# A transformer trunk on one NeuronCore: the last 256 output channels with tokens stationary, and two gate tiles ahead of the second branch

## The chip, the cores and the metric

The kernel runs on one core of a Trainium2 chip. A core has a matrix engine (TensorE, here PE), a vector engine (VectorE, DVE), an engine for functions of one operand (ScalarE, ACT), a general engine (GpSimd, POOL) and a queue engine (SyncE, SP). They share the on-chip memory SBUF; PE writes into the banks of PSUM, which DVE and ACT read. DMA engines move data between DRAM and SBUF; a transfer is issued from the queue of SP, ACT or POOL. The metric is the device time of one execution in microseconds, as the median of several.

## The reference

One layer for 256 tokens of 2048 channels in fp32. A token mixer of three branches comes first, then a gated MLP, then a last RMS norm:

```
h = rms_norm(x, mix_norm)
(u_a, q_b, f_b, i_b, og_b, cx_c, v_c, o_c, ig_c, fg_c, gates) = split(h @ w_in)
y_a = s5_mixer(u_a, ...)                    # state space model, 512 channels
y_b = hgrn2_mixer(q_b, f_b, i_b, og_b, ...) # gated recurrence, 6 heads of 128
y_c = mlstm_mixer(cx_c, v_c, o_c, ...)      # matrix memory, 4 heads of 192
merged = sigmoid(g_a) * (y_a @ w_a) + sigmoid(g_b) * (y_b @ w_b) + sigmoid(g_c) * (y_c @ w_c)
x = x + merged @ w_out
up = causal_dwconv(rms_norm(x, ffn_norm) @ w_up, 3 taps)   # 2 x 5632 channels
x = x + (silu(up[:5632]) * up[5632:]) @ w_down
return rms_norm(x, final_norm)              # x * rsqrt(mean(x*x) + 1e-6) * final_norm
```

## The kernel before

Everything is kept with channels on the 128 partitions and the 256 tokens along the free axis; a channel tile is 128 channels by 256 tokens, and x has 16 of them. Products are made in three parts for precision: each fp32 operand is split into a high and a low part (type fp32r), and high x high, high x low and low x high are summed in a bank. Weights are split on the chip: a job loads up to 2048 columns of a weight matrix into a buffer `raw` (three of them, issued on SP), and each sub-job of up to 1024 columns has its high part `wh` written by ACT (line 117) and its low part `wl` by DVE (line 128), three buffers each. PE multiplies at line 148.

There are two ways round. In `form_a` (line 334) the weights are stationary and the tokens move; the wide form sends both parts of the moving operand past the high weights in one 512-wide product and adds one 256-wide product for the low weights. In `form_b` (line 383) 128 tokens are stationary and the weights move, and the result has tokens on the partitions.

The order of the instructions is written by the program itself: a list of jobs in the order of the calls at the end of `hybrid_trunk` (lines 1535 to 1563), worked through by `run_jobs` (line 271) with the splits two sub-jobs and the loads two jobs ahead. Between pieces of a job a function `pump` (line 223) advances generators, which are the smaller work (norms, recurrences, heads) cut into steps. A clock model `ck` with costs per instruction decides how far they go; it sets the order only. Each engine then works through its own queue in order and waits on semaphores.

In the middle, the names are these. `project_tail` makes the last two token projections (og and o). Behind them come the products of the second branch with its weights `w_bb`: six jobs of two output tiles, each tile one sub-job of 768 columns with 18 products. A gate tile (`gate_tile`, line 1237) is a wide product over 16 channel tiles whose result, times the row factor `R1`, goes through a sigmoid and is kept in a page until the branch is merged; branch b keeps its gates on the pages 8 and 9, and so does branch c after it. Meanwhile the mLSTM generator turns the input and forget gates `gif` into the tile `rows` (Abs, Exp, Ln on ACT, with function tables to load between them), and the four heads follow.

At the end, `w_down_tiles` makes the 16 channel tiles of the down projection, 44 contraction tiles each, tiles 0 to 14 in the wide form and tile 15 with three 256-wide products per contraction tile. Each is added to x; its squares are summed into `ACC` on POOL, and x is multiplied by `final_norm`, all beside the next tile's products. After tile 15, `row_stats` sums the squares over partitions with a product with ones, makes 1/sqrt with Ln, Exp and one Newton step over 256 columns, and `finish` multiplies all 16 tiles by the result in six pieces (three tiles of the last one on POOL) and stores them from the queues of SP and ACT.

## Time and profile before

| | us |
|---|---|
| median of three runs | 1558.77 (1557.72 to 1559.37) |
| the profiled execution | 1557.51 |
| its span in the trace | 1555.7 |
| PE busy in the span | 1533.6 (99%) |
| DVE, ACT, POOL busy | 1085.2, 879.3, 93.0 |

The span runs from the first to the last thing that the trace has; the time of the execution is a little longer. An engine's busy time is that of its instructions, and for a matmul it is a modelled one: a product 256 wide has a record of some 0.28 us, while the next one starts about 0.12 us after it, so start times tell more than lengths. A chain of waits is followed back from the last instruction to whatever released each step. An instruction that waits is listed with the engine and instruction that ended its wait.

### The profile page before, as it was taken

The page shows a single profiled execution, that of the slowest core. Times are in us where ns is not written, and L with a number is a line of the kernel's source. Part 1 is how long each engine was busy: PE and PEld are TensorE (multiplying, and loading weights), DVE is VectorE, ACT ScalarE, POOL GpSimd, SP SyncE. Part 2 cuts the span into 40 slices and gives each one's busy share as a digit, 9 for nine tenths or more (in the row PEclk, how much of TensorE's full clock was granted, in tenths as well). Part 3 has the DMA queues.
Part 4 walks back from the last instruction along what each step waited for, and adds up shares of the span by engine and source line. Part 5 has one row for each costly group of instructions (what it writes and reads, how often), then busy time and mean ns, then how long its engine had stood idle before and what let it go on. Part 6 is the DMA issues. An engine that isn't in the chain of part 4 may idle for free.

```text
span 1555.7 us, 25413 instructions
## 1 busy us (share of the span) xinstructions
PE 1533.6 (99%) x10166; PEld 1398.6 (90%) x10166; DVE 1085.2 (70%) x1668; ACT 879.3 (57%) x1287; POOL 93.0 (6%) x178
## 2 busy tenths in 40 slices
PE   9999999999999999999999999999999999999996
PEld 9999999998899888898888888888888888888886
DVE  7887986778744666686667777777777776545454
ACT  5456666566645477454556555555555555444442
POOL 7400000000000000000110000000000000000010
PEclk9999999999999999999999999999999999999998
DMA  7555454345555524466555555555555555555552
GB/s 306 200 181 168 171 205 163 137 162 179 173 173 193 180 102 173 162 233 217 190 187 184 187 185 187 186 187 190 189 187 190 190 190 183 186 195 180 196 179 99
DMA packets 43014, 285.07 MB, mean 183 GB/s; under 512 B 4944, under 2 KB 5328, under 8 KB 13200
## 3 DMA queue, kind: packets, MB, share of 16 engines
q1 hardware_dynamic: 40464, 274.19, 51.0%
q0 software_dynamic: 1568, 7.28, 1.4%
q10 hardware_dynamic: 864, 2.00, 0.3%
q8 instruction: 79, 1.29, 0.3%
q14 instruction: 39, 0.32, 0.1%
HBM read 281.34 MB, written 2.10 MB: 182 GB/s over the span
## 4 chain that ended last, share of the span: by engine, by line
PE 95%; POOL 2%; DMA 1%; DVE 1%; ACT 1%; issue 1%; DVEq 0%; SPq 0%; ACTq 0%
PE mp L148 90%; PE xp L148 4%; DMA xT<-x 1%; PE xp L157 0%; POOL s_cs L128 0%; ACT wh L117 0%; POOL s5pw L134 0%; DVE wl L128 0%; POOL s_z L128 0%; DVE x L128 0%; POOL s_th L128 0%; POOL s5pw L136 0%; DVEq L1677 0%; POOL xm L134 0%; ACT rows L117 0%
## 5 line engine op out<-in xcount | busy, mean ns | idle before, releaser
L128 DVE TENSOR_TENSOR wl<-raw,wh 128x1024 fp32r<-128x1024 f32 (+2 forms) x534 | 633.8, 1188 | 416.6 <-ACT wh L117 412.6
L117 ACT ACTIVATE wh<-raw 128x1024 fp32r<-128x1024 f32 (+2 forms) x534 | 549.9, 1031 | 613.1 <-PE mp L148 498.7
L148 PE MATMUL mp<-HX,wh 128*128 128x512 f32 (+1 forms) x3072 | 871.6, 353 | 3.1 <-DVE merged L128 1.5
L148 PE MATMUL mp<-HX,wl 128*128 128x256 f32 x2496 | 672.7, 280 | 0.0
L148 PEld LDWEIGHTS mp<-HX,wh 128*128 128x128 f32 x3072 | 527.1, 188 | 79.0 <-issue 2.7
L148 PEld LDWEIGHTS mp<-HX,wl 128*128 128x128 f32 x2496 | 465.8, 188 | 10.2
L148 PE MATMUL mp<-g,wh 128*128 128x512 f32 (+1 forms) x748 | 245.2, 380 | 0.0
L148 PE MATMUL mp<-g,wl 128*128 128x256 f32 x704 | 195.0, 281 | 0.0
L148 PEld LDWEIGHTS mp<-g,wh 128*128 128x128 f32 x748 | 136.4, 188 | 27.4
L148 PE MATMUL mp<-wh,HX 128*128 128x256 f32 (+1 forms) x768 | 139.5, 282 | 0.0
L148 PEld LDWEIGHTS mp<-g,wl 128*128 128x128 f32 x704 | 132.3, 188 | 1.3
L148 PEld LDWEIGHTS mp<-wh,HX 128*128 128x128 f32 x768 | 119.4, 189 | 0.2 <-issue 0.2
L148 PE MATMUL mp<-wl,HX 128*128 128x256 f32 (+1 forms) x384 | 108.1, 281 | 0.5 <-DVE wl L128 0.5
L148 PE MATMUL mp<-m,wh 128*128 128x512 f32 x256 | 88.8, 395 | 0.0
L140 DVE SCALAR_TENSOR_TENSOR upc<-up,cols,upc 128x255 f32<-128x255 f32 (+1 forms) x176 | 84.6, 481 | 3.1
L148 PEld LDWEIGHTS mp<-wl,HX 128*128 128x128 f32 x384 | 72.3, 188 | 0.8 <-DVE wl L128 0.7
L148 PE MATMUL mp<-m,wl 128*128 128x256 f32 x256 | 69.2, 280 | 0.0
L117 ACT ACT_TABLE_LOAD x46 | 59.0, 1283 | 0.8
L117 ACT ACTIVATE upc<-up,cols 128x256 f32<-128x256 f32 x88 | 53.0, 602 | 11.1 <-DVE up L128 11.0
L148 PEld LDWEIGHTS mp<-m,wh 128*128 128x128 f32 x256 | 47.1, 188 | 10.0
L148 PEld LDWEIGHTS mp<-m,wl 128*128 128x128 f32 x256 | 48.1, 188 | 1.3
L128 POOL TENSOR_TENSOR ACC<-ACC,sq 128x256 f32<-128x256 f32 x28 | 33.4, 1194 | 261.4 <-ACT sq L117 261.4
(320 smaller groups left out, 1330.6 us busy)
## 6 DMA issues: line engine op xcount, KB each, us to landing
raw<-w_in SPq DMA_DIRECT2D x88, 1024.0 KB, 4.8
raw<-w_up SPq DMA_DIRECT2D x88, 1024.0 KB, 4.9
raw<-w_down SPq DMA_DIRECT2D x32, 1024.0 KB, 5.0
raw<-w_out SPq DMA_DIRECT2D x16, 1024.0 KB, 4.9
raw<-w_down SPq DMA_DIRECT2D x16, 768.0 KB, 4.2
raw<-w_bb SPq DMA_DIRECT2D x8, 768.0 KB, 4.2
raw<-w_bc SPq DMA_DIRECT2D x8, 768.0 KB, 4.3
raw<-w_ba SPq DMA_DIRECT2D x4, 1024.0 KB, 4.9
```

Of the source, the lines that this page charges most:

```text
L117: nc.scalar.activation(out=out, in_=in_, func=func, **kw)
L128: e.tensor_tensor(out=out, in0=in0, in1=in1, op=op)
L140: nc.vector.scalar_tensor_tensor(out=out, in0=in0, scalar=s, in1=in1, op0=op0, op1=op1)
L148: nc.tensor.matmul(out, lhsT, rhs, start=start, stop=stop)
```

## The change

Two parts. First, the last two channel tiles of the down projection (256 channels) are no longer made with weights stationary. `last_tiles` makes them with tokens stationary: for each of two token tiles one bank of 128 tokens by 256 channels, over 44 contraction tiles with three products each. The weights come in eleven sub-jobs of four contraction tiles; a sub-job marked A is multiplied for both token tiles, one marked R for token tile 0 only, and its split weights are kept in `HH` and `HL` until token tile 0 is complete. The residual x of these channels is added by products with the identity matrix. The squares of the first 14 channel tiles are summed over partitions to one column per token tile (`rest_means`), and the squares of the last 256 channels are summed along the row by ACT. So in `tail` the norm of a token tile is a column of 128 numbers. It multiplies the new channels directly, and a product with the identity spreads it over partitions for the 14 old tiles, which are read from SBUF with this factor from a bank. Each token tile has its own stores; tile 0's tail is a generator among the products left for tile 1. The output array has another layout, and `final_norm` of the last channels comes in as rows (`finr`).

Second, two of branch c's gate tiles stand ahead of the second branch's jobs, the other ten where the twelve stood; branch c's first six gates are on page 15 in place of page 8, and the pages are told apart by branch.

```diff
             if part is None or i == part:
                 nc.sync.dma_start(out=job["raw"][:, c0:c0 + n], in_=job["src"][:, c0:c0 + n])
-    def split(job, c0, n):
+    def split(job, c0, n, to=None):
         raw = job["raw"]
-        wh = sb([P, RAW // 2], F32R, "wh", bufs=3)
-        wl = sb([P, RAW // 2], F32R, "wl", bufs=3)
+        wh = to[0] if to else sb([P, RAW // 2], F32R, "wh", bufs=3)
+        wl = to[1] if to else sb([P, RAW // 2], F32R, "wl", bufs=3)
...
@@ -1242,8 +1242,8 @@
                 if key == "a" and m == 4:
                     yield from wait_for("us2")
                 if (m - 4 if key == "a" else m) % 6 == 0:
-                    merged["page", m // 6] = page(at[m // 6], [P, 6, T], name="gates")
-                s = merged["page", 0 if key == "a" else m // 6][:, m % 6, :]
+                    merged["page", key, m // 6] = page(at[m // 6], [P, 6, T], name="gates")
+                s = merged["page", key, 0 if key == "a" else m // 6][:, m % 6, :]
             merged[key, m] = s
             if wide:
                 total(s, ps)
...
@@ -1411,37 +1411,123 @@
         def evac(m):
             def f(ps):
                 x = v["x"][m // 8][:, m % 8, :]
-                if m < KT - 1:
-                    tt(x, x, ps[:, 0], ADD, after=ck.t["pe"] - 2.6)
-                    tt(x, x, ps[:, 1], ADD)
-                else:
-                    tt(x, x, ps, ADD, after=ck.t["pe"])
-                if m < KT - 1:
-                    yield
-                sq = squares(x, m)
-                if m < KT - 1:
-                    yield
-                    act(x, x, AF.Copy, scale=col("fin", m))
-                else:
-                    yield from row_stats([ACC, sq])
+                tt(x, x, ps[:, 0], ADD, after=ck.t["pe"] - 2.6)
+                tt(x, x, ps[:, 1], ADD)
+                yield
+                squares(x, m)
+                yield
+                act(x, x, AF.Copy, scale=col("fin", m))
+                if m == KT - 3:
+                    gens.append(("r1", rest_means(ck.t["pool"])))
             return f
-        for m in range(KT):
-            form_a(a["w_down"][m], g_parts, evac(m), nk=FT, before=table_for_ln if m == 8 else None, flush=m == 0,
-                   wide=m < KT - 1)
+        for m in range(KT - 2):
+            form_a(a["w_down"][m], g_parts, evac(m), nk=FT, before=table_for_ln if m == 8 else None, flush=m == 0, wide=True)
+        last_tiles()
+    end = {}
+    def rest_means(t):
+        yield from until("pe", t)
+        bank = yield from side()
+        for i in range(NT):
+            mm(bank[:, i:i + 1], ACC[:, i * P:(i + 1) * P], ones[:, 0:1], True, True)
+        yield
+        end["rest"] = small([P, NT], "rest")
+        end["rest_at"] = ts(end["rest"], bank[:, :NT], 1.0 / D, MULT, EPS, ADD, after=ck.t["pe"])
+        shut(bank)
+    def last_tiles():
+        kept, order = [], "AAARARARARA"
+        hi, lo = (x.rearrange("p k t -> p (k t)") for x in (HH, HL))
+        def products(i, k, w_h, w_l, first=False, last=False):
+            ps = end[i]
+            g = [x[:, i * P:(i + 1) * P] for x in (g_parts(k)[:, 0], g_parts(k)[:, 1])]
+            mm(ps, g[0], w_h, first, False)
+            if first:
+                for c in range(2):
+                    mm(ps[:, c * P:(c + 1) * P], v["x"][1][:, 6 + c, i * P:(i + 1) * P], ident, False, False)
+            mm(ps, g[0], w_l, False, False)
+            mm(ps, g[1], w_h, False, last)
+        def sub(n):
+            def fn(wh, wl):
+                if n == 0:
+                    for i in range(NT):
+                        end[i] = main_ps()[:, :T]
+                w = [(4 * n + k, wh[:, k * T:(k + 1) * T], wl[:, k * T:(k + 1) * T]) for k in range(4)]
+                ends = n == len(order) - 1
+                for i in range(NT if order[n] == "A" else 1):
+                    if i:
+                        yield
+                    for j, x in enumerate(w):
+                        products(i, *x, first=n == 0 and j == 0, last=i == 0 and ends and j == 3)
+                    if ends and i == 0:
+                        gens.append(("r1", tail(0, ck.t["pe"])))
+                if order[n] == "R":
+                    kept.extend(w)
+                if ends:
+                    for j, x in enumerate(kept):
+                        yield
+                        products(1, *x, last=j == len(kept) - 1)
+                return []
+            return fn
+        def before():
+            ck.table = TABLES[AF.Ln]
+            end["fin"] = page(15, [P, T], name="finr")
+            nc.gpsimd.dma_start(out=end["fin"], in_=a["finr"])
+        at, n = 0, 0
+        while n < len(order):
+            m = min(2, len(order) - n)
+            job = add_job(a["w_dl"][:, at:at + m * 1024], m * 1024, [(1024 * k, 1024, sub(n + k)) for k in range(m)],
+                          before=before if n == 0 else None)
+            job["to"] = {}
+            for k in range(m):
+                if order[n + k] == "R":
+                    c = order[:n + k].count("R") * 1024
+                    job["to"][k] = (hi[:, c:c + 1024], lo[:, c:c + 1024])
+            at, n = at + m * 1024, n + m
+    def tail(i, t):
+        y = sb([P, RAW], F32, "raw", bufs=3, name="y")
+        ps = end[i]
+        sq, acc, w, r = scratch(name="sq"), small([P, 1], f"acc{i}"), small([P, 1], f"lw{i}"), small([P, 1], f"lr{i}")
+        var = small([P, 1], f"lv{i}")
+        t = act(sq, ps, AF.Square, accum_out=acc, after=max(t, end["rest_at"]))
+        tv = ts(var, acc, 1.0 / D, MULT, end["rest"][:, i:i + 1], ADD, after=t)
+        act(w, acc, AF.Ln, scale=1.0 / D, bias=end["rest"][:, i:i + 1])
+        t = act(r, w, AF.Exp, scale=-0.5)
+        stt(w, r, -0.5, r, MULT, MULT, after=max(t, tv))
+        tt(w, w, var, MULT)
+        t = stt(r, w, 1.5, r, ADD, MULT)
+        queues = (nc.sync, nc.scalar)
+        stt(y[:, D - T:D], ps, r[:, 0:1], end["fin"], MULT, MULT)
+        queues[1].dma_start(out=a["out"][i, :, D - T:], in_=y[:, D - T:D])
+        yield from until("pe", t)
+        bank = yield from side()
+        R = bank[:, :P]
+        mm(R, r[:, 0:1].broadcast_to([P, P]), ident, True, True, after=t)
+        t = ck.t["pe"]
+        at = 0
+        for g, n in enumerate((4, 4, 3, 3) if i == 0 else (2, 3, 3, 4, 2)):
+            o = at % 8
+            tt(y[:, at * P:(at + n) * P].rearrange("p (m t) -> p m t", t=P),
+               v["x"][at // 8][:, o:o + n, i * P:(i + 1) * P], bc(R.unsqueeze(1), [P, n, P]), MULT, after=t)
+            queues[g % 2].dma_start(out=a["out"][i, :, at * P:(at + n) * P], in_=y[:, at * P:(at + n) * P])
+            at += n
+        shut(bank)
     def finish():
-        at = 0
-        for g, n in enumerate((1, 2, 2, 3, 4, 4)):
-            i, o = divmod(at, 8)
-            x = v["x"][i][:, o:o + n, :]
-            if at + n == KT:
-                tt(x[:, :n - 1, :], x[:, :n - 1, :], bc(R1.unsqueeze(1), [P, n - 1, T]), MULT, eng="pool")
-                stt(x[:, n - 1, :], x[:, n - 1, :], col("fin", KT - 1), R1, MULT, MULT)
-            else:
-                tt(x, x, bc(R1.unsqueeze(1), [P, n, T]), MULT)
-            (nc.sync, nc.scalar)[g % 2].dma_start(out=a["out"][:, at:at + n, :], in_=x)
-            at += n
+        drain("r1")
+        gens.append(("r1", tail(1, ck.t["pe"])))
+        drain("r1")
     def first_norm(load_to, split_to):
...
@@ -1548,12 +1634,15 @@
     for m in range(12):
         gate_tile(a["w_in"][n + 16 + m], m, "b", (8, 9), wide=True)
     project_tail(rest, evac_tok)
+    for m in range(2):
+        gate_tile(a["w_in"][n + 32 + m], m, "c", (15, 9), wide=True)
     for g in range(6):
         branch_job(a["w_bb"][g], [2 * g, 2 * g + 1], 6, "b", ["hg"] if g == 0 else None)
     for g in range(6, 8):
         gate_pair("b", n + 16, [2 * g, 2 * g + 1], a["w_bb"][g], 6, None)
-    for m in range(12):
-        gate_tile(a["w_in"][n + 32 + m], m, "c", (8, 9), wide=True)
+    for m in range(2, 12):
+        gate_tile(a["w_in"][n + 32 + m], m, "c", (15, 9), wide=True)
     for g in range(6):
         branch_job(a["w_bc"][g], [2 * g, 2 * g + 1], 6, "c", ["ml"] if g == 0 else None)
     for g in range(6, 8):
...
@@ -1618,7 +1707,10 @@
     o["w_out"] = stationary(np.asarray(i["w_out"])[0])
     up = stationary(np.asarray(i["ffn_w_up"])[0])
     o["w_up"] = up.reshape(2, FT, P, D).transpose(1, 0, 2, 3).reshape(2 * FT, P, D)
-    o["w_down"] = stationary(np.asarray(i["ffn_w_down"])[0])
+    down = np.asarray(i["ffn_w_down"])[0]
+    o["w_down"] = stationary(down[:, :D - T])
+    o["w_dl"] = down[:, D - T:].reshape(FT, P, T).transpose(1, 0, 2).reshape(P, FT * T)
+    o["finr"] = np.broadcast_to(np.asarray(i["final_norm"])[None, D - T:], (P, T))
     qk = np.asarray(i["ml_w_qk"])[0]
     qk = np.concatenate([qk[..., :MD], qk[..., MD + P:], qk[..., MD:MD + P]], axis=-1)
```

Two places in the instruction order. On ACT, around the mLSTM gate steps (`rows`; `ybh` is the second branch's input, `o` a token projection's result, `wh` the split of weights), before:

```order
L117 ACTIVATE ybh<-xp,cols 128x256 x6
L117 ACTIVATE wh<-raw 128x768
L117 ACTIVATE o<-mp,r1c 128x256 x2
L117 ACTIVATE rows<-xp,cols 4x256 x2
L117 ACTIVATE wh<-raw 128x768
L117 ACTIVATE rows<-rows 4x256
L117 ACT_TABLE_LOAD
L117 ACTIVATE rows<-rows 4x256
L117 ACT_TABLE_LOAD
L117 ACTIVATE rows<-rows 4x256
L117 ACTIVATE wh<-raw 128x768 x8
```

and in the changed kernel:

```order
L117 ACTIVATE ybh<-xp,cols 128x256 x6
L117 ACTIVATE wh<-raw 128x1024
L117 ACTIVATE o<-mp,r1c 128x256 x2
L117 ACTIVATE rows<-xp,cols 4x256 x2
L117 ACTIVATE rows<-rows 4x256
L117 ACT_TABLE_LOAD
L117 ACTIVATE rows<-rows 4x256
L117 ACT_TABLE_LOAD
L117 ACTIVATE rows<-rows 4x256
L117 ACTIVATE wh<-raw 128x1024
L117 ACTIVATE wh<-raw 128x768
L117 ACTIVATE gates<-mp 128x256
```

The splits around the gate steps are now those of the gate tiles (1024 columns, eight pairs of products each) where they were those of the branch (768 columns, 18 products each), and one split fewer stands between the copies into `rows` and the steps on it.

On PE, the last rows of the program (`g` is the MLP's hidden state, `ACC` and `sq` the sums of squares), before:

```order
L148 MATMUL mp<-g,wl 128x256
L148 MATMUL mp<-g,wh 128x256 x2
L148 MATMUL mp<-g,wl 128x256
L148 MATMUL xp<-ACC,ones 128x256
L148 MATMUL xp<-sq,ones 128x256
L1677 UNCONDITIONAL_BRANCH
```

and in the changed kernel, where the weights kept in `HX` (`HH` and `HL`) move and `lr` is the column of row factors:

```order
L148 MATMUL mp<-wl,g 128x256
L148 MATMUL mp<-wh,g 128x256 x2
L148 MATMUL mp<-wl,g 128x256
L148 MATMUL mp<-wh,g 128x256
L148 MATMUL mp<-HX,g 128x256 x12
L148 MATMUL xp<-ident,lr_15440 128x128
L148 MATMUL mp<-HX,g 128x256 x36
L148 MATMUL xp<-ident,lr_15525 128x128
L1769 UNCONDITIONAL_BRANCH
```

Token tile 0 is complete 12 products ahead of the first row of `HX` here (the twelve in between are token tile 1's with the last sub-job's weights); the spreading of its factor stands behind 24 of tile 1's products and ahead of 36.

## Rows read from the trace of the kernel before

**Rows 1.** The first section of the page (busy time of each engine, its share of the span, instructions) and the shares by engine of the chain that ended last.

```profile
PE 1533.6 (99%) x10166; PEld 1398.6 (90%) x10166; DVE 1085.2 (70%) x1668; ACT 879.3 (57%) x1287; POOL 93.0 (6%) x178
...
PE 95%; POOL 2%; DMA 1%; DVE 1%; ACT 1%; issue 1%; DVEq 0%; SPq 0%; ACTq 0%
```

**Rows 2.** Busy time by stretch. Columns: stretch and its length in us; busy us (and instructions) of PE, PEld (the weight load), DVE, ACT, POOL; granted clock of PE; busy share of the DMA engines; GB/s.

```profile
1510.30:1525.70 15.40, 15.40 (x89) 13.47 (x88) 7.59 (x9) 6.64 (x8) 1.40 (x1) 1.00 0.57 189
1525.70:1541.20 15.50, 15.50 (x134) 15.49 (x133) 6.11 (x7) 4.52 (x6) 1.40 (x1) 1.00 0.00 0
...
1541.20:1555.70 14.50, 1.28 (x6) 0.48 (x4) 7.75 (x11) 1.31 (x3) 1.98 (x1) 0.62 0.38 145
503.73:515.36 11.63, 9.66 (x80) 9.18 (x77) 4.75 (x10) 9.31 (x16) 2.39 (x5) 1.00 0.45 149
```

**Rows 3.** Four pieces of the chain that ended last, behind the last product: start in us, length in us, engine, what it writes, line.

```profile
1541.90 0.42 ACT sq L117
...
1542.37 0.71 PE xp L148 x2
...
1543.17 0.48 ACT rw L117
...
1543.74 0.42 DVE var L136
```

**Rows 4.** Single instructions in order of time, on PE at 477.69, 514.37, 515.36 and 545.98 and on ACT from 509.71: start us, us, engine, line, operation, written<-read, count, and in brackets the idle time before it and what ended it.

```profile
477.69 0.39 PE L148 MATMUL xp<-V,sc 128*128 128x128 f32 x2
...
514.37 0.38 PE L148 MATMUL mp<-ybh,wh 128*128 128x256 f32 x1 [1.48 <-ACT wh L117]
...
515.36 0.38 PE L148 MATMUL mp<-ybh,wl 128*128 128x256 f32 x1 [0.49 <-DVE wl L128]
...
545.98 0.45 PE L148 MATMUL xp<-rows,mlw 128*128 128x256 f32 x1 [0.77 <-issue]
...
509.71 0.42 ACT L117 ACTIVATE rows<-rows 4x256 f32<-4x256 f32 x1 [2.07 <-DVE rows L134]
...
513.17 0.41 ACT L117 ACTIVATE rows<-rows 4x256 f32<-4x256 f32 x1
```

**Rows 5.** Instructions in order of time at the end of the program, the same columns.

```profile
1541.07 0.28 PE L148 MATMUL mp<-g,wl 128*128 128x256 f32 x1
...
1541.39 0.42 DVE L128 TENSOR_TENSOR x<-x,mp 128x256 f32<-128x256 f32 x1 [5.75 <-PE mp L148]
...
1545.56 2.63 DVE L128 TENSOR_TENSOR x<-x,R 128x256 f32<-128x256 f32 x2
...
1545.90 2.29 DVE L128 TENSOR_TENSOR x<-x,R 128x512 f32<-128x512 f32 x1
...
1548.11 1.55 DVE L128 TENSOR_TENSOR x<-x,R 128x512 f32<-128x512 f32 x2
...
1548.71 2.08 DVE L128 TENSOR_TENSOR x<-x,R 128x768 f32<-128x768 f32 x2
...
1551.28 0.34 ACTq L1443 DMA_DIRECT2D out_dram<-x  x1
```

**Rows 6.** Pieces of the same chain further ahead, where it runs along PE: start, length, engine, bank written, line, records.

```profile
473.00 1.34 PE xp L148 x12
...
478.52 21.22 PE mp L148 x180
...
535.29 0.34 PE xp L157 x4
...
537.22 5.18 PE xp L148 x24
```

**Rows 7.** Groups of instructions of one shape from 1345 to 1541 (the second half of the down projection): line, engine, operation, written<-read, shapes, count | busy us, mean ns of one | idle before, released by.

```profile
L128 DVE TENSOR_TENSOR wl<-raw,wh 128x1024 fp32r<-128x1024 f32 x62 | 76.0, 1226 | 82.6 <-ACT wh L117 82.6
L117 ACT ACTIVATE wh<-raw 128x1024 fp32r<-128x1024 f32 x61 | 64.7, 1060 | 89.4 <-PE mp L148 55.7 <-issue 17.7 <-DVE x L128 16.0
```

**Rows 8.** Instructions in order of time in an mLSTM head, on ACT (from 603.34) and on DVE (from 570.09): operations two columns wide, and a Square with a sum along the row with the read of its accumulator.

```profile
603.34 0.20 ACT L117 ACTIVATE mlr_w<-mls 128x2 f32<-128x2 f32 x1
603.58 0.20 ACT L117 ACTIVATE mlr_r<-mlr_w 128x2 f32<-128x2 f32 x1
603.69 0.31 ACT L117 ACTIVATE junk<-xp 128x192 f32<-128x192 f32 x1
603.90 0.19 ACT L117 ACTIVATION_READ_ACCUMULATOR junk<-xp 128x1 f32 x1
...
570.09 0.16 DVE L128 TENSOR_TENSOR mlr_w<-mlr_w,mls 128x2 f32<-128x2 f32 x1
570.28 0.16 DVE L140 SCALAR_TENSOR_TENSOR mlr_r<-mlr_w,mlr_r 128x2 f32<-128x2 f32 x1
```

**Rows 9.** DMA issues of the output: written<-read, queue, count, KB each, us from issue to landing.

```profile
out_dram<-x ACTq DMA_DIRECT2D x1, 512.0 KB, 3.5
...
out_dram<-x SPq DMA_DIRECT2D x1, 256.0 KB, 2.2
...
out_dram<-x SPq DMA_DIRECT2D x1, 128.0 KB, 1.7
```

**Rows 10.** Groups of one shape from 1541 to 1556, columns as in rows 7: a Vector operation with one operand in a bank (mp) and one with both in SBUF.

```profile
L128 DVE TENSOR_TENSOR x<-x,R 128x256 f32<-128x256 f32 x1 | 0.4, 424 | 0.0
L128 DVE TENSOR_TENSOR x<-x,mp 128x256 f32<-128x256 f32 x1 | 0.4, 421 | 5.8 <-PE mp L148 5.8
```

More of the change, by code (lines that the diff above doesn't have):

```diff
@@ L287, in split_to @@
                 c0, n, _ = job["subs"][k]
-                parts[len(parts)] = split(job, c0, n)
+                parts[len(parts)] = split(job, c0, n, job.get("to", {}).get(k))
         def step_all(its):
@@ L1580 @@
 _NAMES = ("x", "cols", "ident", "ij", "hmask", "cmask", "sel", "s5b", "s5bl", "s5c", "w_in", "w_vg", "w_glu", "w_qk",
-          "w_ba", "w_bb", "w_bc", "w_out", "w_up", "w_down")
+          "w_ba", "w_bb", "w_bc", "w_out", "w_up", "w_down", "w_dl", "finr")
 def _layouts(i):
@@ L1675 @@
     aps = {n: nc.dram_tensor(n, x.shape, mybir.dt.from_np(x.dtype), kind="ExternalInput").ap() for n, x in arrays.items()}
-    aps["out"] = nc.dram_tensor("out_0_dram", (P, KT, T), F32, kind="ExternalOutput").ap()
+    aps["out"] = nc.dram_tensor("out_0_dram", (NT, P, D), F32, kind="ExternalOutput").ap()
     with tile.TileContext(nc) as tc:
@@ L1680 @@
     got = r.results[0]["out_0_dram"]
-    return np.ascontiguousarray(got.transpose(1, 0, 2).reshape(D, T).T)[None]
+    first = got[:, :, :D - T].reshape(NT, P, -1, P).transpose(0, 3, 2, 1).reshape(T, D - T)
+    return np.concatenate([first, got[:, :, D - T:].reshape(T, T)], axis=1)[None]
```

## The prediction

> **What bounds the kernel now.** I read the page first: of 1555.7 us TensorE (PE) is busy 1533.6, and the chain that ended last is PE for 95% [rows 1]. So only three things can shorten this kernel: fewer PE products, less waiting of PE inside the span, and a shorter stretch behind the last product. Next came busy time by stretch [rows 2]: from 1525.70 to 1541.20 PE is busy without a gap, and from 1541.20 to the end it is busy 1.28 of 14.50 us. That stretch is the first place the change touches. The second is 503.73 to 515.36 [rows 2], with PE busy 9.66 of 11.63 us. Third, the chain of waits at the end [rows 3], to see what the 14.5 us are made of: addition of the last tile, square, sum over partitions, Ln, Exp, three Vector steps, six multiplications, stores. Fourth, PE and ScalarE (ACT) in order of time around 513 [rows 4], to see what PE waits for there.
>
> I count the tail from the start of the last product, 1541.07 [rows 5]: 1555.70 − 1541.07 = **14.63 us**. The profiled execution itself took 1557.51, so 1.81 lie around its span, and the median of the three runs, 1558.77, is 1.26 above it. I take the difference in the profile and put it on the median.
>
> **PE's work in the last two channel tiles.** Before, tile 14 is made of pairs (a 512-wide and a 256-wide product) and tile 15 of 132 products 256 wide: 15.40 and 15.50 us in their stretches [rows 2], together 30.9. After, 44 contraction tiles x 2 token tiles x 3 = 264 products, with tokens stationary and 256 channels moving. That form runs before in the token projections: 180 products in 21.22 us, 0.118 each [rows 6]. 264 x 0.1179 = 31.1, so **+0.24**. Four identity products bring the residual into the bank; a full-fp32 product of 128x128 leaves two records, and twelve records (six products) take 1.34 us, 0.223 each [rows 6]: 4 x 0.223 = **+0.9**. The two products that sum ACC are one column wide; the nearest rows are four records of 4x4 transposes in 0.34 us and 0.223 for a 128x128 product [rows 6], so 0.34 to 0.45: **+0.4**. Tile 0's broadcast of its row factor is one more 128x128 product: **+0.22**. Sum **+1.76**; if each of these seven fp32 products showed the whole 0.39 us that its two records span [rows 4], and the broadcast waited a little, it would be 3.0; at best 1.2.
>
> Does PE wait at tile 0's broadcast? In the order it stands 24 products (2.83 us) behind tile 0's last one. The chain up to it, worked out below, takes 2.0 us. It is covered, with 0.8 us to spare. Tile 0's four multiplications and five stores then lie under the 36 products left (4.2 us) and under tile 1's own chain; what they would cost uncovered is the price of rival 3. The weights feed this stage faster than the one before: a pair of sub-jobs (one for both token tiles, one for tile 0 alone) is used up in 36 x 0.118 = 4.2 us instead of 5.6, which asks for 1 MB (1.05 million bytes) per 4.2 us = 248 GB/s against the 189 of the stage before [rows 2]. In those 4.2 us ACT has two splits of 1.06 and VectorE (DVE) two of 1.23 [rows 7], and the split runs two sub-jobs ahead. I cost it at nothing; SP and the POOL queue carry nothing else there but one 128 KB load.
>
> **The tail of tile 1**, from the start of the last product. +0.32 until a reader of the bank starts (1541.07 to 1541.39 [rows 5]). Square with a sum along the row: 0.42 for 256 wide [rows 3], and the accumulator's read ends 0.08 behind a Square [rows 8]: 0.50. Ln and Exp on one column: 0.24 apart [rows 8], 0.48. To DVE 0.09 (1543.65 to 1543.74 [rows 3]); three one-column steps at 0.19 [rows 8], 0.57. To PE 0.05 (1542.32 to 1542.37 [rows 3]), broadcast product and its way to DVE 0.45 (two records in 0.39 [rows 4]). Sum 2.46; the multiplication of the 256 new channels stands on DVE during the broadcast and is hidden by it. Then five multiplications of 256, 384, 384, 512 and 256: start to start 0.34 for 256 (1545.56 to 1545.90) and 0.60 for 512 (1548.11 to 1548.71) [rows 5], so 0.47 for 384; 0.34 + 0.47 + 0.47 + 0.60 + 0.42 = 2.30. At 4.76 the last store may go; 0.09 to its issue, as from ACT to DVE above. It has 128 KB; landings were 1.7 for 128 KB, 2.2 for 256 KB and up to 3.5 for 512 [rows 9]. The store before it (256 KB) is 0.5 us older, so I take 2.0. From the last landing to the end of the span: 1555.70 − (1551.28 + 3.5) = 0.92 [rows 5, 9]. Sum 2.46 + 2.30 + 0.09 + 2.0 + 0.92 = **7.77 us** against 14.63: **−6.86**.
>
> What makes the old tail long, and goes: the 256-wide rows of the norm (seven operations of 0.42 to 0.47 where now one column is enough), multiplications over 2 MB of output against 7/8 of 1 MB, and a DVE multiplication of 512 that took 2.29 us [rows 5], beside one of 768 on POOL, while the next of that size passed in 0.60, start to start. After, POOL has nothing in the tail. Bounds: with the landing at 1.7, 7.46; with a landing of 3.5 and the five one-column steps at 0.42 like wide ones (+1.05), 10.3. Gain 4.3 to 7.2; I stay at 6.86, since the rows used are of the same kind and nearly the same size.
>
> The trace has a Vector operation of 256 with one operand in a PSUM bank at 0.421 and with both in SBUF at 0.424 [rows 10], so I add nothing for the row factor being read from a bank. [...]
>
> **The middle.** Before, PE waits 1.48 for ACT's split of the next weights until 514.37, and again 0.49 for DVE's half: 1.48 + 0.49 = 1.97 [rows 4]. ACT was late because the mLSTM gate steps (five activations and two table loads of 1.28, 509.71 to 513.58) stand ahead of that split, while PE uses up a 768-wide split in 2.13 us. After, two gate tiles (4 sub-jobs of 2.8 us) run there. Let t be the start of their first product. The transposes for the gate rows come 1.4 behind it and take 0.35; the way to ACT and its two row copies (a 256-wide step takes 0.42) until 2.8; DVE's step with its waits 0.35; the five ACT steps 3.87 (509.71 to 513.58): 7.1. Then the split of the fourth sub-job, 1.06, and DVE's half, 1.23: 9.4. PE wants it at 0.35 + 3 x 2.8 = 8.75 and its DVE half 0.23 later: a wait of 0.4. So **−1.5**. What is late next: the 12 branch splits of 2.13 us with the head work of ACT beside them. There PE has 5.2 us of fp32 products of its own [rows 6] against some 3 us of copies on ACT between two splits, so no wait of weight; 0.77 was lost there before, at 545.98 [rows 4]. Bounds: 0 (the wait returns later) to 2.7 (1.97 + 0.77).
>
> The other 11.2 us of PE work of these two tiles are only moved, and the page change lets the third branch's gates start without the second's being used up; neither is on the path.
>
> **Sum.** −6.86 + 1.76 − 1.5 = **−6.6 us**: profiled execution 1550.9, median 1558.77 − 6.6 = **1552.2**.
>
> **Rivals.**
> 1. *The wait in the middle moves.* The heads now stand beside narrow branch splits, and 1.97 us are lost there in pieces. For it: ACT is busy 9.31 of 11.63 us in that stretch [rows 2]. Against: the hand count above. Then 1558.77 − 5.1 = 1553.7. Chance 0.18.
> 2. *The tail is bound by the stores.* 1 MB in six pieces: if the last lands 3.5 us after issue and small steps cost double, the gain of the tail is 4.3, in all 4.3 − 1.76 + 1.5 = 4.0: 1554.7. For it: 512 KB took 3.5 with others in flight [rows 9]. Against: half the bytes, spread from 2.4 us on. Chance 0.10. [...] The largest store that a row here shows has 512 KB.
> 3. *Tile 0's tail is not hidden.* If its chain exceeds 2.83 us, PE stops at the broadcast, which stands in its queue ahead of 36 products, and each us beyond costs one. With one-column steps at 0.42 it takes 3.05 and costs 0.2; if it took twice what I count, 4.0, it costs 1.2: 1553.4. This is also the case in which the change does not do what it says. Chance 0.05.
> 4. *Slower: the heads starve PE.* With the second branch's narrow splits, each of the four mLSTM heads puts its table loads (1.28 each) and copies ahead of a split as the gate steps did at 513, at about 2 us. If PE waits there for more than 6.6 + 1.5 = 8.1 us in sum, the kernel gets slower; four heads with two such places each would be 16 us, less the 5.1 of the tail: +10.9, 1569.7. Against: before, the same heads cost 0.77 us in one place [rows 4], and part of them lay beside narrow splits too. Chance 0.05.
>
> **Chances and range.** The forecast has 0.62, with its own range 1550.5 to 1554. What can be told from no change is about 0.2%, 3.1 us, so faster means below 1555.6. The forecast, rivals 1 and 3 and over half of rival 2 lie there: 0.88; within 0.2% (the bad end of rival 2, some of rival 4): 0.07; slower 0.05. Adding all bounds gives a gain of 4.3 − 3.0 + 0 = 1.3 to 7.2 − 1.2 + 2.7 = 8.7; cut to 8 in 10 and widened by the spread of the three runs (1.65), 1549.6 to 1555.6.
>
> **What would show it.** In the changed profile: last product to end of span 7.3 to 8.3 us; the stretch of the last stage about 1.8 us longer on PE, without idle time at tile 0's broadcast; no POOL work in the tail; PE's idle time between 503 and 516 under 0.8. The prediction is wrong if the last store lands over 3 us behind its issue, if PE shows waits for splits between 515 and 560, or if the 264 products run slower than 0.12 us each.

## The result, and the profile after

The changed kernel takes **1550.29 us**, the median of four runs (1550.07 to 1550.68); the kernel before took 1558.87 in the same session (1557.72 to 1559.37). The ratio is 0.9947, 95% interval 0.9934 to 0.9960. That is 8.6 us less, where 6.6 were forecast. The two profiled executions differ by less: spans of 1548.5 and 1555.7, 7.2 us. Where the other 1.4 lie is the subject of two of the experiments. Two executions took far longer, one of the kernel before (2239 us) and the traced one of `tail_only` (3504 us); they are left out, so `tail_only` has times and no trace.

First the page's busy times and chain, which answer to [rows 1]:

```profile
span 1548.5 us, 25513 instructions
...
PE 1534.1 (99%) x10222; PEld 1401.9 (91%) x10222; DVE 1083.5 (70%) x1674; ACT 875.8 (57%) x1286; POOL 89.5 (6%) x177
...
PE 95%; POOL 2%; DMA 1%; DVE 1%; ACT 1%; issue 0%; SPq 0%; DVEq 0%; ACTq 0%
```

PE still bounds it, with 0.5 us more work in a span 7.2 us shorter. Next, busy time by stretch (columns as in [rows 2]): the middle in two pieces, the last stage, and what lies behind the last product.

```profile
500.00:516.00 16.00, 15.56 (x102) 13.82 (x101) 8.90 (x16) 13.96 (x23) 2.39 (x5) 1.00 0.35 126
516.00:560.00 44.00, 44.00 (x315) 41.93 (x315) 30.98 (x67) 24.06 (x47) 0.00 (x0) 1.00 0.48 163
1507.53:1540.45 32.92, 32.91 (x279) 32.70 (x277) 15.77 (x22) 10.89 (x15) 1.07 (x1) 1.00 0.34 113
1540.45:1548.50 8.05, 0.49 (x2) 0.30 (x2) 3.46 (x10) 0.97 (x4) 0.00 (x0) 0.75 0.37 130
```

The same two stretches of the middle in the kernel before:

```profile
500.00:516.00 16.00, 14.02 (x117) 13.52 (x116) 7.88 (x15) 11.93 (x21) 2.39 (x5) 1.00 0.44 148
516.00:560.00 44.00, 43.23 (x300) 40.40 (x300) 30.49 (x54) 24.42 (x39) 0.00 (x0) 1.00 0.45 155
```

PE's idle time fell from 1.98 to 0.44 and from 0.77 to 0: 2.31 us. Then the tail in order of time, which answers to [rows 5] (columns as there):

```profile
1539.80 0.64 PE L148 MATMUL mp<-HX,g 128*128 128x256 f32 x4
...
1540.54 0.38 ACT L117 ACTIVATE sq<-mp 128x256 f32<-128x256 f32 x1 [6.32 <-PE mp L148]
...
1541.04 0.29 ACT L117 ACTIVATE lw<-acc,rest 128x1 f32<-128x1 f32 x1
...
1541.61 0.16 DVE L140 SCALAR_TENSOR_TENSOR lw<-lr 128x1 f32<-128x1 f32 x1 [0.35 <-ACT lr L117]
...
1542.21 0.49 PE L148 MATMUL xp<-ident,lr 128*128 128x128 f32 x2 [1.77 <-DVE lr L140]
...
1542.73 2.28 DVE L128 TENSOR_TENSOR y<-x,xp 128x256 f32<-128x256 f32 x5
...
1545.04 0.33 SPq L1523 DMA_DIRECT2D out_dram<-y  x1
```

The last of the four products in the first row starts 0.28 ahead of their common end, at 1540.16; from there to the end of the span are 8.34 us, where 14.63 were before. So the profiles add up: the last stage starts 2.77 earlier (1507.53 for 1510.30), takes 1.86 more (32.63 for 30.77), and the tail is 6.29 shorter: −7.2.

### The profile page after: what moved, and what is told of

Read it like the earlier page. It is cut to its first block, busy times and chain, and to the rows that moved or that the text cites. A ratio compares the mean times of both kernels' runs of the same rounds, so it can differ in the third digit from the quotient of the medians.

```text
span 1548.5 us, 25513 instructions
## 1 busy us (share of the span) xinstructions
PE 1534.1 (99%) x10222; PEld 1401.9 (91%) x10222; DVE 1083.5 (70%) x1674; ACT 875.8 (57%) x1286; POOL 89.5 (6%) x177
## 4 chain that ended last, share of the span: by engine, by line
PE 95%; POOL 2%; DMA 1%; DVE 1%; ACT 1%; issue 0%; SPq 0%; DVEq 0%; ACTq 0%
PE mp L148 91%; PE xp L148 4%; DMA xT<-x 1%; PE xp L157 0%; POOL s_cs L128 0%; POOL s5pw L134 0%; POOL s_z L128 0%; DVE wl L128 0%; ACT wh L117 0%; POOL s_th L128 0%; POOL xm L134 0%; DVE y L128 0%; SPq L208 0%; POOL s5pw L136 0%; ACT L117 0%
## 5 line engine op out<-in xcount | busy, mean ns | idle before, releaser
L148 PE MATMUL mp<-g,wh 128*128 128x512 f32 x616 | 214.6, 394 | 0.0
L148 PE MATMUL mp<-g,wl 128*128 128x256 f32 x616 | 170.5, 281 | 0.0
L148 PEld LDWEIGHTS mp<-g,wh 128*128 128x128 f32 x616 | 114.8, 188 | 25.6
L148 PEld LDWEIGHTS mp<-g,wl 128*128 128x128 f32 x616 | 115.8, 188 | 1.2
```

Of the source, the lines that this page charges most:

```text
L148: nc.tensor.matmul(out, lhsT, rhs, start=start, stop=stop)
```

## The experiments

The kernel before ran 49 times beside these runs: 30 took 1557.3 to 1558.0 and 19 took 1558.8 to 1559.2, with nothing between. I call these the lower and the upper group.

### Each half alone

`tail_only` is the changed kernel with the old order of the gate tiles:

```diff
-    for m in range(2):
-        gate_tile(a["w_in"][n + 32 + m], m, "c", (15, 9), wide=True)
...
-    for m in range(2, 12):
-        gate_tile(a["w_in"][n + 32 + m], m, "c", (15, 9), wide=True)
+    for m in range(12):
+        gate_tile(a["w_in"][n + 32 + m], m, "c", (8, 9), wide=True)
```

> Theory: the two parts of the change add up and do not touch each other; the gate tiles bring 2.8 us, the tail the rest. Then this kernel, which has the new tail and the old order of the gates, takes 2.8 us more than the changed one: about 1553.1 (1552.5 to 1553.8). In its profile PE is idle for about 2 us between 503 and 516 and 0.77 again near 546, the last stage and the tail look as in the changed kernel (8.3 us from the last product to the end). Rival: the middle's gain is given back later or comes from something else; then it stays within 0.5 us of the changed kernel, at 1550 to 1550.8.

`gates_only` is the old kernel with this edit the other way round.

> Theory: 2.8 us less than before, some 1556.1 (1555.4 to 1556.8), with the old tail of 14.6 us unchanged and PE's idle time at 514 and 546 gone. Rival: the gate tiles help only together with the new tail, or the wait returns later: 1558.3 to 1559.

Measured: `tail_only` 1554.4, three runs at 1553.0 to 1553.7 and four at 1554.4 to 1555.2, ratio 0.9972 (0.9961 to 0.9983). `gates_only` 1554.72 in one group (1554.5 to 1555.5), ratio 0.9978 (0.9969 to 0.9987). Both medians fell outside the ranges I had written: that of `gates_only` because I had started from 1558.87, a median out of the upper group, that of `tail_only` because it lies among its upper runs, while the three lower ones are inside. From the lower group, 1557.5, it fits: 1557.5 − 2.8 = 1554.7; the lower times of `tail_only`, 1553.1, are 4.4 less; and 1557.5 − 2.8 − 4.4 = 1550.3 is the changed kernel. The halves add up. And the upper group is there with the old order of the gates and gone with the new one, whichever tail stands behind it. Two reservations: in `tail_only` the groups are only 0.7 apart, and of the 57 runs here with the new order one stands 1.5 above the rest of its kernel (1551.67, in `short_norm` below), for a reason that no trace shows.

### Where the upper group comes from

`old_filled` is the old kernel with idle products in the pause:

```diff
                     ps = main_ps()[:, :T]
+                    if (key, m) == ("b", 4):
+                        for _ in range(12):
+                            nc.tensor.matmul(ps, yh[:, 0, :P], yh[:, 0, :], start=True, stop=True)
```

> The old kernel with 12 idle products (1.4 us, results overwritten) ahead of the product that waits at 514.37, so that TensorE works where it waited 1.48 us; nothing else is moved. Theory (clock): with the pause down to 0.49 and some tenths the granted clock stays at full speed in every execution; the upper group of times near 1559 goes, all runs lie at 1557.3 to 1557.9, median 1557.5. Rival (the two groups come from elsewhere): two groups remain, 1.5 us apart, in about the old shares. Rival (the products are not hidden): 1.4 us more, 1558.9 and up.

Measured: 1557.49, eleven runs from 1557.4 to 1558.2, none in the upper group; ratio 0.9997 (0.9988 to 1.0005). Busy time by stretch shows the mechanism. The kernel before, an execution of the lower group:

```profile
512.70:516.00 3.30, 1.32 (x9) 0.94 (x8) 1.61 (x3) 3.08 (x5) 0.00 (x0) 1.00 0.00 0
516.00:520.00 4.00, 4.00 (x36) 4.00 (x36) 3.93 (x8) 1.25 (x2) 0.00 (x0) 1.00 0.48 163
```

`before_dve` (below), which has the same middle, in an execution of its upper group (of the kernel before itself none of that group was traced):

```profile
512.70:516.00 3.30, 1.32 (x9) 0.91 (x9) 1.57 (x3) 3.12 (x5) 0.00 (x0) 1.00 0.00 0
516.00:520.00 4.00, 4.00 (x24) 4.00 (x23) 3.93 (x8) 0.84 (x1) 0.00 (x0) 0.57 0.43 149
...
517.00:518.00 1.00, 1.00 (x6) 1.00 (x6) 0.97 (x4) 0.00 (x0) 0.00 (x0) 0.50 0.00 0
```

And `old_filled`:

```profile
512.70:516.00 3.30, 2.75 (x21) 2.35 (x20) 1.67 (x4) 3.02 (x5) 0.00 (x0) 1.00 0.00 0
516.00:520.00 4.00, 4.00 (x36) 4.00 (x35) 3.93 (x8) 1.30 (x2) 0.00 (x0) 1.00 0.48 161
```

After the same 1.98 us of waiting PE ran on at a granted clock of 1.00 in one execution, and at 0.50 for some 3 us in another: 24 products in 4 us where 36 fit, 12 x 0.118 = 1.4 us lost. With 12 products put into the pause the clock stayed at 1.00 in the traced execution, and all eleven runs were of the lower group, which 30 in 49 would give by chance about once in 200. What decides in one execution or the other is not in the trace.

### GpSimd in the old tail

`before_dve` gives the last three channel tiles of the old tail to VectorE:

```diff
-                tt(x[:, :n - 1, :], x[:, :n - 1, :], bc(R1.unsqueeze(1), [P, n - 1, T]), MULT, eng="pool")
+                tt(x[:, :n - 1, :], x[:, :n - 1, :], bc(R1.unsqueeze(1), [P, n - 1, T]), MULT)
```

> The old kernel with the last three tiles' multiplication on VectorE in place of GpSimd. Theory A (GpSimd's piece slowed VectorE: one multiplication of 512 took 2.29 in place of 0.60 beside it): VectorE then has 16 tiles at 0.26 to 0.3 each, 4.7 us in place of 5.6, and the kernel is 0.8 us faster than before, 1558.1; no multiplication of 512 takes over 0.7. Theory B (the GpSimd piece took work off VectorE): 768 more elements on VectorE cost 0.8, so 1559.7. And if the spread of the old kernel's runs (1.65 us) comes from that piece, these runs lie within 0.8 us of each other.

Measured: 1555.85, groups at 1555.6 to 1555.9 and 1557.3 to 1557.6, ratio 0.9989 (0.9980 to 0.9998). The sign is theory A's, but it is twice as much: 1.6 to 1.7 less in either group. The spread is not from this piece (above). From the last product to the end of VectorE's work it went from 10.12 us to 9.38, 0.74 less as expected; to the end of the span from 14.63 to 13.0. The stores account for the rest. The first large one is issued 7.15 us behind the start of the last product in the kernel before and 5.54 in `before_dve`, where that product starts 1.53 later: 1.61 less, nearly as much as the span's 1.63.

```profile
1548.22 1.82 ACTq L1443 DMA_DIRECT2D out_dram<-x  x2
```

```profile
1542.60 0.28 PE L148 MATMUL mp<-g,wl 128*128 128x256 f32 x1
...
1548.14 1.82 ACTq L1443 DMA_DIRECT2D out_dram<-x  x2
```

Busy time by stretch behind it, again the kernel before and then `before_dve`:

```profile
1548.00:1549.00 1.00, 0.00 (x0) 0.00 (x0) 1.00 (x3) 0.00 (x0) 0.00 (x0) 0.50 0.00 0
1549.00:1554.00 5.00, 0.00 (x0) 0.00 (x0) 2.19 (x3) 0.00 (x0) 0.00 (x0) 0.50 0.97 374
```

```profile
1548.00:1549.00 1.00, 0.00 (x0) 0.00 (x0) 1.00 (x3) 0.00 (x0) 0.00 (x0) 0.50 0.39 133
1549.00:1554.00 5.00, 0.00 (x0) 0.00 (x0) 2.98 (x4) 0.00 (x0) 0.00 (x0) 0.50 0.97 380
```

The DMA engines (last but one column) are full for 5 us in both. So the old tail ended when 2 MB had gone out at 374 to 380 GB/s, counted from the first large store, and that store waited for the multiplication that took 2.29 us beside GpSimd's [rows 5]; without it the two of that size took 0.68 each. The 3.5 us that a 512 KB store took to land [rows 9] I read as time in line, which the traces don't show for a single store.

VectorE's slowness beside GpSimd is measured, 2.29 against 0.68 us; what in the chip causes it no trace here shows.

### Is tile 0's place in the order worth anything?

`no_replay`, with the same 264 products:

```diff
-        kept, order = [], "AAARARARARA"
+        kept, order = [], "AAAAAAAAAAA"
...
-                        products(i, *x, first=n == 0 and j == 0, last=i == 0 and ends and j == 3)
+                        products(i, *x, first=n == 0 and j == 0, last=(i == 0 or not kept) and ends and j == 3)
```

> The changed kernel with both token tiles' products side by side to the end, so that only 12 products (1.5 us) lie behind tile 0's last one in place of 60 (7.3 us); the number of products is the same. Theory: tile 0's chain (2.0 us to its row factor, 3.3 to its first multiplication, 2.2 for the four) is then no longer hidden, and since its stores stand on ScalarE's queue ahead of tile 1's square, the square waits until tile 0's last multiplication is done: 1538.65 + 3.3 + 2.2 + 0.35 is about 1544.4 in place of 1540.5, so +3.4 to +3.9, 1553.7 to 1554.2. Rival 3 of the prediction as it was priced there (only PE's stop at the broadcast counts, 2.0 less 1.4): +0.6, 1550.9. Rival: the place of tile 0's chain does not matter: within 0.3 of the changed kernel.

Measured: 1553.73 (1553.4 to 1554.0), ratio 0.9972 (0.9961 to 0.9983): 3.4 more than the changed kernel, as the theory has it. ScalarE and PE in order of time:

```profile
1543.79 0.38 ACT L117 ACTIVATE sq<-mp 128x256 f32<-128x256 f32 x1 [3.85 <-DVE y L128]
```

```profile
1540.58 0.49 PE L148 MATMUL xp<-ident,lr 128*128 128x128 f32 x2 [0.39 <-DVE lr L140]
1545.46 0.80 PE L148 MATMUL xp<-ident,lr 128*128 128x128 f32 x2 [4.40 <-DVE lr L140]
```

PE's stop at tile 0's broadcast is only 0.39, as rival 3 of the prediction would have it. But tile 1's Square could start at 1540.3 (0.38 behind the start of the last product at 1539.91, as in the changed kernel) and starts at 1543.79: on ScalarE's queue it stands behind tile 0's stores, and these wait for VectorE (`y`). Its broadcast then runs at a granted clock of 0.50, 0.80 us for 0.49. So the rival was under-priced: uncovered, tile 0 costs 3.4 us and not 0.6 to 1.2.

### How many gate tiles

`gates_1` and `gates_4` put 1 and 4 ahead of the second branch in place of 2 (`range(1)` and `range(1, 12)`; `range(4)` and `range(4, 12)`). `after_again` is the changed kernel beside `gates_1`.

> The changed kernel once more, beside the others of this group. All theories: 1550.3, since the old kernel's lower group of times (1557.3 to 1557.7) less 2.8 in the middle and 4.4 in the tail is 1550.3. Theory (clock): its runs form one group within 0.8 us, while the old kernel's fall into two, near 1557.5 and 1559.0, because the old wait of 2 us at 514 is followed in some executions by some 3 us at half the TensorE clock and the remaining 0.44 is not. Rival (noise of the chip): the changed kernel's runs spread over 1.5 us too.

> One gate tile ahead of the second branch in place of two. Theory (the wait is the gate steps' time less what TensorE has in hand; a gate sub-job gives it 2.8 us, a branch sub-job 2.13): the third of the three sub-jobs in hand is 0.67 shorter, so the wait near 513 is 0.44 + 0.67 = 1.1 and the kernel takes 1551.0, plus up to 1.5 in those executions where the clock falls. Rival (any sub-job ahead of the branch helps as much): 1550.3 within 0.3.

> Four gate tiles ahead of the second branch. Theory (what counts is that VectorE's row step and ScalarE's gate steps start soon after the transposes; from one gate tile on they do, and the 0.44 left is the split that stands behind them): no change, 1550.3 within 0.3, PE's wait near 513 again 0.4 to 0.5. Rival (more work in hand for TensorE shortens the wait further): the 0.44 goes, 1549.9.

Measured: `after_again` 1550.33 (1550.2 to 1550.5), ratio 0.9948 (0.9934 to 0.9962), one group; `gates_1` 1550.16 (1549.9 to 1550.3), 0.9947 (0.9934 to 0.9959); `gates_4` 1551.22 (1551.2 to 1551.4), 0.9957 (0.9943 to 0.9970). My theory failed for both of the latter. In `gates_1` PE waits 0.40 and not 1.1. The reason is what stands ahead of VectorE's row step, on which ScalarE's gate steps wait. VectorE in the kernel before:

```profile
507.68 0.96 DVE L128 TENSOR_TENSOR wl<-raw,wh 128x768 fp32r<-128x768 f32 x1 [1.14 <-ACT wh L117]
508.55 0.42 DVE L128 TENSOR_TENSOR gates<-mp,gates 128x256 f32<-128x256 f32 x1
509.00 0.42 DVE L128 TENSOR_TENSOR merged<-merged,gates 128x256 f32<-128x256 f32 x1
509.34 0.28 DVE L134 TENSOR_SCALAR rows<-rows 4x256 f32<-4x256 f32 x1
```

In `gates_1`, and in the changed kernel:

```profile
508.55 0.27 DVE L134 TENSOR_SCALAR rows<-rows 4x256 f32<-4x256 f32 x1
```

```profile
506.96 0.27 DVE L134 TENSOR_SCALAR rows<-rows 4x256 f32<-4x256 f32 x1
```

Before, the row step stood behind the merging of the first branch tile (two steps of 0.42) and started 5.6 us after the transposes that feed it (503.73); in `gates_1` it is 3.7 behind them, in the changed kernel 1.8. With the gate tiles in front there is nothing to merge yet. In `gates_1` one split more than in the changed kernel also passes ahead of the gate steps. So the gain is not only work in hand for PE, as I had counted it.

In `gates_4` the wait at 513 is 0.44 again, as the theory said, but 0.77 are back, at the product that stood at 545.98 before [rows 4]. ScalarE there, and in the changed kernel at the same copies:

```profile
533.92 0.67 PE L148 MATMUL xp<-rows,mlw 128*128 128x256 f32 x2 [0.77 <-issue]
```

```profile
530.32 0.85 ACT L117 ACTIVATE wh<-raw 128x768 fp32r<-128x768 f32 x1 [5.21 <-PE mp L148]
531.19 1.28 ACT L117 ACT_TABLE_LOAD   x1
532.48 0.42 ACT L117 ACTIVATE gates<-gates 128x256 f32<-128x256 f32 x1
532.80 2.75 ACT L117 ACTIVATE qk<-xp 128x256 f32<-128x256 f32 x8
```

```profile
524.91 1.45 ACT L117 ACTIVATE qk<-xp 128x256 f32<-128x256 f32 x4 [0.95 <-PE xp L148]
```

The copies of a head's query and key (`qk<-xp`) free banks of PE. In `gates_4`, and likewise before, they stand behind a split that waits on ScalarE for 5 us (6 before) until PE frees a weight buffer; in the changed kernel they follow PE's products at once. The trace names no releaser for the 0.77, so this is the likely reading and not a shown one. If it holds, that part of the gain is an accident of the order.

### The price of single steps

`no_ident` leaves out the identity products:

```diff
-            if first:
-                for c in range(2):
-                    mm(ps[:, c * P:(c + 1) * P], v["x"][1][:, 6 + c, i * P:(i + 1) * P], ident, False, False)
```

> The changed kernel without the four products by the identity, so the residual of the last 256 channels is left out of the output. This prices them alone: the prediction has 0.9 us for the four; by the spacing of the changed kernel's trace (two of them take 0.36 from start to start of what follows) it is 0.72 to 0.9. Theory (TensorE is the bound of this stage, everything on it is paid): 1549.4 to 1549.6, the stage 31.8 in place of 32.6 us. Rival (the stage is held by the splits, so products are free): 1550.3.

Measured: 1549.37 (1549.2 to 1549.7), ratio 0.9946 (0.9933 to 0.9958), 0.96 less than `after_again`. Its stage runs from 1507.86 to 1539.60, 31.74 us: 0.89 less. They are paid in full.

`short_norm` takes one VectorE step out of the chain (`end["half"]` is −0.5 times `rest`, made ahead):

```diff
-        tv = ts(var, acc, 1.0 / D, MULT, end["rest"][:, i:i + 1], ADD, after=t)
+        tv = ts(var, acc, -0.5 / D, MULT, end["half"][:, i:i + 1], ADD, after=t)
...
-        stt(w, r, -0.5, r, MULT, MULT, after=max(t, tv))
-        tt(w, w, var, MULT)
+        stt(w, r, var[:, 0:1], r, MULT, MULT, after=max(t, tv))
```

> The changed kernel with one VectorE step less in each token tile's chain (the factor -0.5 is put into the variance, which is ready earlier). Theory (the chain from the last product to the first multiplication is all on the path, step by step): 0.19 us less in the tail, 1550.1. Rival (the tail is bound by the stores' landing or VectorE's other work): no change, 1550.3. Differences of 0.2 us can be told apart in the profile, by the distance from the last product to the first multiplication (2.57 now, 2.38 by theory), rather than in the times.

`late_start` cuts tile 1's stores otherwise: `(4, 4, 3, 3)` for `(2, 3, 3, 4, 2)`.

> The changed kernel with tile 1's stores cut as 4, 4, 3, 3 channel tiles in place of 2, 3, 3, 4, 2. Theory A (the end is set by the DMA engines, which are full from 1544.5 to 1546.5 in the changed kernel: 1 MB at some 370 GB/s from the moment the first large store starts): the first multiplication is 0.26 to 0.3 longer, so the stores start later and the kernel takes 0.2 to 0.3 more, 1550.5 to 1550.6. Theory B (the end is set by VectorE, which issues the last store at 2.3 us behind the first multiplication's start): one instruction less, 0.05 us less, with a last store of 192 in place of 128 KB: 1550.3. The profile tells them apart: last issue to the end of the span (3.46 in the changed kernel) grows under A.

`best` puts `gates_1`, `short_norm` and stores of `(1, 3, 4, 4, 2)` together.

> One gate tile, the chain of the norm shorter by one step, and tile 1's stores cut as 1, 3, 4, 4, 2 so that the first starts 0.13 earlier. Theory: the parts add, 0.17 (gate tile) + 0.3 (step, as timed) + up to 0.1 under theory A of the stores: 1549.8 in place of 1550.33. Rival (the end is set by VectorE alone, the rest was noise): 1550.0 to 1550.2.

Measured: `short_norm` 1550.01 (1549.9 to 1551.7), 0.9948 (0.9935 to 0.9960); `late_start` 1550.36 (1550.2 to 1550.8), 0.9952 (0.9939 to 0.9964); `best` 1550.15 (1549.8 to 1550.4), 0.9950 (0.9937 to 0.9962). From Square to the first multiplication `short_norm` has 2.07 where the changed kernel has 2.19: 0.12 and not 0.19, since the step with the column as a factor takes 0.06 more. From Square to the end of the span it is 7.96 in the changed kernel, 7.78 in `short_norm`, 8.22 in `late_start`, 7.88 in `best`. So `late_start`'s later stores cost 0.26 in its trace, and from its last issue, 1544.72, to the end are 3.8 where the changed kernel has 3.46, both as theory A says; its time shows nothing of it, and `best`, whose first store goes earlier, gained nothing by that. Theory A is supported and not settled. The DMA engines in the changed kernel:

```profile
1543.50:1544.50 1.00, 0.00 (x0) 0.00 (x0) 1.00 (x3) 0.00 (x0) 0.00 (x0) 0.99 0.80 263
1544.50:1546.50 2.00, 0.00 (x0) 0.00 (x0) 0.51 (x2) 0.00 (x0) 0.00 (x0) 0.50 1.01 362
```

`best` came out where its rival had it; the parts did not add. It lies 0.2 below the changed kernel, which is about the spread of either, and the 0.5 by which its traced span is shorter is mostly not its edits' work: 0.35 are there at 468 us already, ahead of all that they move. The changed kernel, then `best`, at the same product:

```profile
468.68 0.38 PE L148 MATMUL xp<-V,sc 128*128 128x128 f32 x2
```

```profile
468.33 0.38 PE L148 MATMUL xp<-V,sc 128*128 128x128 f32 x2
```

So no version here beats the changed kernel clearly, and differences of 0.2 to 0.3 us between single traces tell little, unless they are counted inside one stage.

## Why the prediction was right, and where it was off

The measured 1550.29 lies in the stated range, 1549.6 to 1555.6, and 0.2 below the forecast's own, 1550.5 to 1554. In the profile two misses partly cancel: the middle brought 1.3 us more than forecast and the tail 0.57 less, so −7.2 came out for −6.6. The rest is a term that the prediction did not have, in the median. How its added bounds (a gain of 1.3 to 8.7) became the stated range can't be redone from what it says.

**PE's last stage.** Forecast +1.76, measured +1.86. The identity products were put at 0.9 and cost 0.89. Tile 0's broadcast caused no wait (1535.77, without a bracket), as said. The stage was not held by splits.

```profile
1535.77 0.38 PE L148 MATMUL xp<-ident,lr 128*128 128x128 f32 x2
```

**The tail of tile 1.** Forecast 7.77, measured 8.34. To the first multiplication 2.57 (forecast 2.46), the five multiplications 2.28 (2.30), and 0.03 to the last issue (0.09). Nearly all of the miss is behind the last issue: 3.46 for 2.0 + 0.92, and 8.34 is just outside the 7.3 to 8.3 given as a sign. The failing terms are "so I take 2.0" and the 0.92 taken over from the old tail, which came out as 2.3 and 1.16. The first store of 128 KB on SP's queue landed in 1.8, the last in 2.3, with the DMA engines full from 1544.5 to 1546.5:

```profile
out_dram<-y SPq DMA_DIRECT2D x1, 128.0 KB, 1.8
...
out_dram<-y SPq DMA_DIRECT2D x1, 128.0 KB, 2.3
```

So rival 2 (bound by the stores) had the right mechanism for the tail's last part, at 0.5 us and not 2.6. What made the old tail long was named in part only: of the 6.3 us gained, up to 1.6 are GpSimd's piece (`before_dve`); 1.9 are the shorter chain to the first multiplication, 4.49 before [rows 5] and 2.57 now; and the 2.8 left are about what 1 MB less takes at 374 GB/s. The last two are worked out, no run takes them apart.

The multiplications that read a bank took 2.28 where the rows gave 2.30, so no cost of the bank shows, as the prediction has it. Behind the last issue the stores cost 0.5 more than I counted, with the engines at 362 GB/s; that stores of the same size landed in 1.8 and 2.3 speaks for the queue and against the size.

**The middle.** Forecast −1.5 with bounds of 0 and −2.7, measured −2.8, just beyond them. The hand count for the wait itself held: 0.44 where 0.4 was forecast.

```profile
513.40 0.38 PE L148 MATMUL mp<-HX,wl 128*128 128x256 f32 x1 [0.44 <-DVE wl L128]
```

The step that failed is leaving the 0.77 at 545.98 in; it went (−1.54 − 0.77 = −2.31 of idle time). Most of the remaining 0.5 is in the brackets themselves, which count from the end of the record before. From start to start the three pauses before [rows 4] took 1.76, 0.77 and 1.06 us, less 0.12 each without a pause; the one in the changed kernel took 0.85, less the 0.24 that follows a 512-wide product. That is 3.23 − 0.61 = 2.6. The products ahead of them, before and in the changed kernel:

```profile
512.61 0.28 PE L148 MATMUL mp<-ybh,wl 128*128 128x256 f32 x1
...
514.59 0.28 PE L148 MATMUL mp<-ybl,wh 128*128 128x256 f32 x1
...
544.92 0.28 PE L148 MATMUL mp<-HX,wl 128*128 128x256 f32 x1
```

```profile
512.20 0.40 PE L148 MATMUL mp<-HX,wh 128*128 128x512 f32 x1
512.44 0.28 PE L148 MATMUL mp<-HX,wl 128*128 128x256 f32 x1
512.55 0.40 PE L148 MATMUL mp<-HX,wh 128*128 128x512 f32 x1
```

The 0.2 left are not traced. The count also did not see why the gate steps came sooner (VectorE's row step, above).

**The median.** The step "I take the difference in the profile and put it on the median" hid a term. The profiled execution was of the lower group, the median of the upper, and the change does away with the upper group: 1.35 us that no row of one execution could show. Against the lower group the gain is 7.2, and 6.6 were forecast; without that term the median would have been 1551.6.

**The rivals.** The wait did not move (1), PE did not stop (3), the heads did not starve PE (4: 44.00 of 44.00 us busy from 516 to 560). Two slips on record change no result: the gate steps are three activations and two table loads, and rival 4 would turn the kernel slower from 5.1 + 1.97 = 7.1 us of waiting on.

## What to carry to other kernels

Look at several times before taking the profiled execution as the kernel: two groups of times with one trace from each can show a cost, here the clock after a pause of 2 us, that no row of a single profile has. When a step is uncovered, price not only the engine that stops but everything queued behind it: stores on ScalarE's queue held the next tile's Square for 3.5 us. At the end of a program ask from when on the DMA engines are full. In the old tail the first large store went 1.6 us earlier in `before_dve` and the end came as much earlier; in the changed kernel an earlier first store brought nothing that the times show (`best`).

## What the runs showed of the hardware

After 1.98 us of waiting in one place PE's granted clock was 0.50 for some 3 us in one traced execution and 1.00 in another; by their times, 19 of 49 executions were of the first kind, at a cost of 1.4 to 1.5 us. With 0.39 to 0.55 us of waiting at that place the clock stayed at 1.00 in every profile here. A VectorE multiplication of 512 with both inputs in SBUF took 2.29 us beside one of GpSimd and 0.68 alone. In the stretches of 2 and 5 us shown, stores to memory kept the DMA engines at a busy share of 0.97 to 1.01, at 362 to 380 GB/s.
